# Norms of the RWKV keys by block-of-ones matmuls, in a hybrid RWKV-7 and MoBA layer on one core

## The chip, the cores and the metric

The kernel runs on one core of one Trainium2 chip. The metric is the device time of one execution in microseconds, as the median of the runs. Engines are named as the profile names them: PE is TensorE's matmuls and PEld its weight loads, DVE is VectorE, ACT is ScalarE, POOL is GpSimd, SP is SyncE.

## The reference, cut to what matters

One decoder layer on 256 tokens of width 2048: a shared RMS norm, one input projection of 12416 columns, two token mixers side by side, two gated projections back to 2048, an output projection and a residual. The change lies in the RWKV-7 mixer, which has 16 heads of 64 channels. Its keys are scaled and normalised per head:

```python
    kk = (k * k_k).reshape(B, S, H, N).astype(f32)
    kk = kk / jnp.maximum(jnp.sqrt(jnp.sum(kk * kk, axis=-1, keepdims=True)), 1e-12)
    k = k * (1.0 + (a - 1.0) * k_a)
    ...
    bh = kk * ah
    ...
    def step(state, inp):
        r_t, w_t, k_t, v_t, kk_t, b_t = inp
        sa = jnp.einsum('bhvk,bhk->bhv', state, -kk_t)
        state = (state * w_t[:, :, None, :]
                 + sa[..., None] * b_t[:, :, None, :]
                 + v_t[..., None] * k_t[:, :, None, :])
        y_t = jnp.einsum('bhvk,bhk->bhv', state, r_t)
        return state, y_t
```

## The kernel before

**Main work.** Every projection is a product of an fp32 weight with activations that are held as two fp32r parts, xh and xl. A weight half of 128 x 1024 is split on the fly: ScalarE copies it to fp32r (hi, L216), VectorE subtracts that from the original (lo, L222), and TensorE does three passes, hi with xh, hi with xl, lo with xh. Channel-major chunks (mm_fm, L314) take 24 matmuls of 256 columns for a weight half, token-major chunks (mm_tm, L334; the queries, keys and values of MoBA) 12 of 512 columns. A job is one weight half. The loop run_jobs (L253) prepares the halves two jobs ahead; hi and lo have three buffers each, and the raw weights two buffers of two halves.

**Side work.** After each job, pump (L199) advances generators that hold everything else: the RWKV elementwise work (rwkv_elem, L405), the score matmuls (rwkv_r, L511), the inversion of triangular 32 x 32 blocks on VectorE (inverse, L557), the state recursion (rwkv_v), attention (moba). The 16 heads are worked in two groups g of 8; tiles have channels on the partitions, two heads to a tile of 128, four tiles fi for a group, and 256 tokens in the columns. The first jobs are ordered by hand (L294); for all the rest a scheduler of the tile framework decides the order of each engine's instructions when the program is built. At run time every engine works strictly in that order.

**The key norms (L453 to L509).** kk is k times k_k (L459), and sq its square (L461), in the first half of a tile named bk (sn in the code). Eight matmuls take 128 columns of sq as weights and a two-column selector sel2 as the moving side (L467), which gives sums with tokens on the partitions, 128 x 16. Square root (L469), maximum (L470) and reciprocal (L471) run on these 16 columns. A copy spreads each norm over 64 columns (L473) in the second half of the tile, eight transposes turn that back to channels on the partitions (L481), and kk is multiplied by it from PSUM (L485). Then ar is kk times a decay (L490), t1 and k follow (L494, L497), a becomes -kk a (L499), and a new tile of the same slot, bk, is filled: one half by VectorE from a (L507), the other by GpSimd from k (L508). The score matmuls (L534) take bk and ar. head_sums (L396) is a helper that sums over heads with a block-diagonal matrix of ones, bones, and leaves each sum on all 64 channels; before, only rwkv_tr used it (L633, matmuls at L401).

Of the kernel before, what the change touches and what calls it, by code (L numbers as in the profile page):

```python
# [10 lines left out]
F32R = mybir.dt.float32r  # L11
BF16 = mybir.dt.bfloat16
U8 = mybir.dt.uint8
AF = mybir.ActivationFunctionType
ALU = mybir.AluOpType
AX = mybir.AxisListType

P = 128
D = 2048
S = 256  # L20
# [16 lines left out]
def tile_hybrid_block(ctx: ExitStack, tc: tile.TileContext, x, pv, wdu, wau,  # L37
                      w_in, w_pr, w_pm, w_out, out):
    nc = tc.nc
    act, dve, pool, pe, sp = nc.scalar, nc.vector, nc.gpsimd, nc.tensor, nc.sync  # L40
# [10 lines left out]
    def nm(s):  # L51
        cnt[0] += 1
        return f"{s}_{cnt[0]}"

    def T(tag, shape, dt=F32, bufs=1):
        return sb.tile(shape, dt, tag=tag, name=nm(tag), bufs=bufs)
# [4 lines left out]
    def PSS():  # L61
        return psd.tile([P, 512], F32, tag="ps", name=nm("ps"))

    def C(name, shape, dt=F32):
        return cp.tile(shape, dt, tag=name, name=name)

    def f32(ap):
        return ap.bitcast(F32)
# [12 lines left out]
    ident = C("ident", [P, P])  # L81
# [23 lines left out]
    pool.memset(mone[0:64, 0:64], 1.0)  # L105
    pool.memset(mone[64:128, 64:128], 1.0)
    dve.tensor_copy(bones, mone)
    sel2 = C("sel2", [P, 2])
    pool.memset(sel2, 0.0)
    pool.memset(sel2[0:64, 0:1], 1.0)  # L110
    pool.memset(sel2[64:128, 1:2], 1.0)
    rst = C("rst", [P, 16, 65], BF16)
    pool.memset(rst, 1.0)
    pool.memset(rst[:, :, 0:1], 0.0)
# [281 lines left out]
    def head_sums(ps, parts, half):  # L396

        for i in range(2):
            fs = slice((2 * half + i) * S, (2 * half + i + 1) * S)
            for u in range(2):  # L400
                pe.matmul(ps[:, i * S:(i + 1) * S], bones, parts[u][:, fs], start=(u == 0),  # L401
                          stop=(u == 1))


    def rwkv_elem(g):  # L405
        r = R[g]
        lr = T("ep", [P, 2, 512])
        for i, src in enumerate((wdu, wau)):
            for sl in (slice(0, 64), slice(64, 128)):
                act.dma_start(lr[sl, i, :], src[:, g * 512:(g + 1) * 512])  # L410
        yield
        yield
        th = T("bk", [P, 2, 512], F32R)
        lw = T("lora", [P, 2, 512], F32R)
        act.activation(th[64:128], lr[64:128], AF.Copy)
        act.activation(lw[0:64], lr[0:64], AF.Copy)
        dve.tensor_tensor(lw[64:128], lr[64:128], f32(th[64:128]), ALU.subtract)
        yield
        sg = T("sg", [P, 4, 4, 65])
        a = T("a", [P, 4, S])  # L420
        pool.memset(sg[:, :, :, 0:1], 0.0)
        for half in range(2):
            pw, pa = PSS(), PSS()
            for i in range(2):
                fi = 2 * half + i
                col = 4 * g + fi
                fs = slice(fi * P, (fi + 1) * P)
                for j, ps in enumerate((pw, pa)):
                    o = ps[:, i * S:(i + 1) * S]
                    pe.matmul(o, lw[:, j, fs], xx[:, 2 * j, :], start=True, stop=False)  # L430
                    pe.matmul(o, lw[:, j, fs], xx[:, 2 * j + 1, :], start=False, stop=True)
                act.activation(sg[:, fi, :, 1:65],
                               pw[:, i * S:(i + 1) * S].rearrange("p (c t) -> p c t", c=4),
                               AF.Sigmoid, bias=PV[:, PV_W0 + col:PV_W0 + col + 1])
                act.activation(a[:, fi, :], pa[:, i * S:(i + 1) * S], AF.Sigmoid,
                               bias=PV[:, PV_A0 + col:PV_A0 + col + 1])
            yield
        cs = T("cs", [P, 16, 65])
        dve.tensor_tensor_scan(cs.rearrange("p a b -> p (a b)"), rst.rearrange("p a b -> p (a b)"),
                               sg.rearrange("p f c t -> p (f c t)"), 0.0, ALU.mult, ALU.add)  # L440
        yield
        cc = T("sg", [P, 16, 65])
        dve.tensor_tensor(cc, cs, cs[:, :, 32:33].to_broadcast([P, 16, 65]), ALU.subtract)
        yield
        ep = T("ep", [P, 4, 4, 65])
        em = T("cs", [P, 4, 4, 65])
        act.activation(ep.rearrange("p f c t -> p (f c) t"), cc, AF.Exp, scale=-LAM)
        act.activation(em.rearrange("p f c t -> p (f c) t"), cc, AF.Exp, scale=LAM)
        fac = T("fac", [P, 4, 3])
        dve.tensor_tensor(fac, ep[:, :, 0:3, 64], em[:, :, 1:4, 0], ALU.mult)  # L450
        r["fac"] = fac
        yield
        k = r["k"]  # L453
        kk = T("kk", [P, 4, S])
        sn = T("bk", [P, 2, 1024])
        sq = sn[:, 0, :].rearrange("p (f t) -> p f t", f=4)
        for fi in range(4):
            col = 4 * g + fi
            dve.tensor_scalar(kk[:, fi, :], k[:, fi, :], PV[:, PV_KK + col:PV_KK + col + 1], None,  # L459
                              ALU.mult)  # L460
        act.activation(sq, kk, AF.Square)  # L461
        yield
        pn = PSS()
        pn4 = pn[:, 0:16].rearrange("p (c f e) -> p c f e", c=2, f=4)
        for c in range(2):
            for fi in range(4):
                pe.matmul(pn4[:, c, fi, :], sq[:, fi, c * P:(c + 1) * P], sel2, start=True, stop=True)  # L467
        n = T("n", [P, 16])
        act.activation(n, pn[:, 0:16], AF.Sqrt)  # L469
        dve.tensor_scalar(n, n, 1e-12, None, ALU.max)  # L470
        dve.reciprocal(n, n)  # L471
        nx = sn[:, 1, :].rearrange("p (a b) -> p a b", b=64)
        dve.tensor_copy(nx, n.rearrange("p (a o) -> p a o", o=1).to_broadcast([P, 16, 64]))  # L473
        yield
        yield
        for half in range(2):
            pb = PSS()
            for i in range(2):
                fi = 2 * half + i
                for c in range(2):  # L480
                    pe.transpose(pb[:, i * S + c * P:i * S + (c + 1) * P],  # L481
                                 nx[:, c * 8 + 2 * fi:c * 8 + 2 * fi + 2, :].rearrange(
                                     "p a b -> p (a b)"), ident)
            v = kk[:, 2 * half:2 * half + 2, :].rearrange("p f t -> p (f t)")
            dve.tensor_tensor(v, v, pb, ALU.mult)  # L485
        yield
        ar = T("ar", [P, 4, 4, 2, 64])
        r["ar"], r["ep"] = ar, ep
        kk4 = kk.rearrange("p f (c t) -> p f c t", c=4)
        dve.tensor_tensor(ar[:, :, :, 0, :], kk4, ep[:, :, :, 0:64], ALU.mult)  # L490
        t1 = sq
        for fi in range(4):
            col = 4 * g + fi
            dve.tensor_scalar(t1[:, fi, :], a[:, fi, :], -1.0, PV[:, PV_KA + col:PV_KA + col + 1],  # L494
                              ALU.add, ALU.mult)
        yield
        dve.scalar_tensor_tensor(k, t1, 1.0, k, ALU.add, ALU.mult)  # L497
        yield
        dve.scalar_tensor_tensor(a, kk, -1.0, a, ALU.mult, ALU.mult)  # L499
        yield  # L500
        bk = T("bk", [P, 4, 4, 2, 64])
        r["bk"] = bk
        a4 = a.rearrange("p f (c t) -> p f c t", c=4)
        k4 = k.rearrange("p f (c t) -> p f c t", c=4)
        for p in range(2):
            sl = slice(64 * p, 64 * p + 64)
            dve.tensor_tensor(bk[sl, :, :, p, :], a4[sl], em[sl, :, :, 1:65], ALU.mult)  # L507
            pool.tensor_tensor(bk[sl, :, :, 1 - p, :], k4[sl], em[sl, :, :, 1:65], ALU.mult)  # L508
            yield  # L509
# [513 lines left out]
    for g in range(2):  # L1023
        c = 512 * g
        chunk(w_in, C_K + c, 512, KT, fm_x, shift_post("k", "k", g, PV_MUK, 8))
        post = shift_post("r", "r", g, PV_MUR, 0)
        if g == 0:
            chunk(w_in, C_WD, 128, KT, fm_x, then(wa_post, (rwkv_elem(0), "e0")))
        else:
            post = then(post, (rwkv_elem(1), "e1"))  # L1030
        chunk(w_in, C_R + c, 512, KT, fm_x, then(post, (rwkv_r(g), f"r{g}")))
        vp = then(shift_post("v", "v", g, PV_MUV, 16), (rwkv_mid(g), f"i{g}"), (rwkv_v(g), f"v{g}"))
        chunk(w_in, C_V + c, 512, KT, fm_x, with_need("v0", vp) if g else vp)
        qp = qk_post("q", g)
        chunk(w_in, C_Q + c, 512, KT, tm_x, with_need("m0", qp) if g else qp)
        chunk(w_in, C_KQ + c, 512, KT, tm_x, qk_post("k", g))
        chunk(w_in, C_VQ + c, 512, KT, tm_x, then(vq_post(g), (moba(g), f"m{g}")))
# [63 lines left out]
```

## Time and profile before

| | |
|---|---|
| median of 3 runs | 836.4 us (835.27 to 838.43) |
| profiled execution | 836.63 us |
| its span, first to last instruction | 834.9 us |
| granted TensorE clock, mean | 0.998 |
| PE, PEld | 98%, 91% of the span |
| DVE, ACT, POOL | 66%, 51%, 3% of the span |

A row of the profile names a source line, an engine, an operation, and out<-in with tile names; times are in microseconds, the mean of one instruction in ns. Matmuls are pipelined, so that a single one shows a longer time than the distance to the next. In brackets stands how long the engine sat idle before and what released it.

### The profile page before, as it was taken

The numbers are of one execution on the slowest core, as the hardware profiler recorded it, in microseconds if no ns is written. First come the engines' busy times: TensorE is split into PE (matmuls) and PEld (weight loads), VectorE is DVE, ScalarE is ACT, GpSimd is POOL, SyncE is SP. The second block draws the span as 40 slices with busy tenths as digits, with TensorE's granted clock in tenths as the row PEclk, the third lists the DMA queues.
The fourth block names the chain that finished last, engine by engine and source line by source line (L and its number), as shares of the span: only waits on it lengthen the run. The fifth ranks groups of instructions, "written<-read, shape, count | busy, mean of one in ns | idle before, by whom it ended". The sixth has DMA issues, their size and how long they took to land.

```text
span 834.9 us, 15904 instructions
## 1 busy us (share of the span) xinstructions
PE 821.7 (98%) x6770; PEld 763.3 (91%) x6770; DVE 550.3 (66%) x776; ACT 423.4 (51%) x568; POOL 28.9 (3%) x42
## 2 busy tenths in 40 slices
PE   8999999999999999999989999999999999999998
PEld 8999878899998788899989998899999999998887
DVE  5769958956569649769955578644554566665553
ACT  6785435544437576445434467654444444443332
POOL 5001200000000002000000000000000000000000
PEclk9999999999999999999999999999999999999999
DMA  8564555664434444455673324566555555556772
GB/s 305 179 199 153 178 163 165 201 177 153 150 108 142 158 152 152 156 173 187 200 220 105 106 98 151 177 202 198 186 184 193 201 186 169 201 176 203 249 231 99
DMA packets 83207, 145.78 MB, mean 175 GB/s; under 512 B 11568, under 2 KB 13872, under 8 KB 83136
## 3 DMA queue, kind: packets, MB, share of 16 engines
q1 hardware_dynamic: 71584, 138.55, 51.2%
q10 hardware_dynamic: 11520, 6.16, 2.7%
q8 instruction: 53, 0.87, 0.4%
q14 instruction: 18, 0.15, 0.1%
q0 software_dynamic: 32, 0.05, 0.0%
HBM read 141.61 MB, written 3.15 MB: 173 GB/s over the span
## 4 chain that ended last, share of the span: by engine, by line
PE 92%; ACT 3%; DVE 2%; DMA 2%; issue 1%; SPq 0%; ACTq 0%; DVEq 0%
PE pm L329 56%; PE pm L348 9%; PE pm L347 9%; PE pm L349 9%; PE ps L534 1%; PE ps L672 1%; PE ps L679 1%; ACT bk L849 1%; PE ps L878 1%; DMA td<-kk 1%; DMA cs<-td 1%; PE ps L831 1%; PE ps L696 1%; DVE lo L222 1%; ACT hi L216 1%
## 5 line engine op out<-in xcount | busy, mean ns | idle before, releaser
L222 DVE TENSOR_TENSOR lo<-raw,hi 128x1024 fp32r<-128x1024 f32 (+1 forms) x259 | 316.3, 1225 | 212.9 <-ACT hi L216 212.0
L216 ACT ACTIVATE hi<-raw 128x1024 fp32r<-128x1024 f32 (+1 forms) x259 | 272.6, 1055 | 339.1 <-PE pm L329 193.1
L329 PE MATMUL pm<-xh,hi 128*128 128x256 f32 x1168 | 326.8, 282 | 0.4 <-ACT xh L144 0.4
L329 PE MATMUL pm<-xl,hi 128*128 128x256 f32 x1168 | 324.9, 280 | 0.0
L329 PE MATMUL pm<-xh,lo 128*128 128x256 f32 x1168 | 323.9, 280 | 1.0 <-DVE lo L222 1.0
L329 PEld LDWEIGHTS pm<-xh,hi 128*128 128x128 f32 x1168 | 220.4, 190 | 3.2 <-issue 0.8
L329 PEld LDWEIGHTS pm<-xh,lo 128*128 128x128 f32 x1168 | 220.0, 190 | 2.6 <-DVE lo L222 1.4
L329 PEld LDWEIGHTS pm<-xl,hi 128*128 128x128 f32 x1168 | 220.8, 190 | 1.0 <-issue 0.3
L348 PE MATMUL pm<-lo,xh 128*128 128x512 f32 x192 | 76.3, 397 | 0.0
L349 PE MATMUL pm<-hi,xl 128*128 128x512 f32 x192 | 75.5, 393 | 0.0
L347 PE MATMUL pm<-hi,xh 128*128 128x512 f32 x192 | 74.1, 401 | 0.0
L348 PE MATMUL pm<-lo,mgh 128*128 128x512 f32 (+1 forms) x128 | 48.4, 378 | 0.0
L349 PE MATMUL pm<-hi,mgl 128*128 128x512 f32 (+1 forms) x128 | 48.0, 376 | 0.0
L347 PE MATMUL pm<-hi,mgh 128*128 128x512 f32 (+1 forms) x128 | 44.4, 377 | 0.0
L349 PEld LDWEIGHTS pm<-hi,xl 128*128 128x128 f32 x192 | 36.1, 188 | 7.8 <-issue 0.2
L348 PEld LDWEIGHTS pm<-lo,xh 128*128 128x128 f32 x192 | 36.1, 188 | 7.7 <-DVE lo L222 0.6
L347 PEld LDWEIGHTS pm<-hi,xh 128*128 128x128 f32 x192 | 35.9, 188 | 7.8 <-issue 0.5
L347 PEld LDWEIGHTS pm<-hi,mgh 128*128 128x128 f32 x128 | 24.0, 188 | 4.7
L349 PEld LDWEIGHTS pm<-hi,mgl 128*128 128x128 f32 x128 | 24.0, 188 | 4.7
L348 PEld LDWEIGHTS pm<-lo,mgh 128*128 128x128 f32 x128 | 24.0, 188 | 4.4
L566 DVE TENSOR_TENSOR tmp<-sg,kk 64x31 f32<-64x31 f32 (+15 forms) x62 | 20.6, 331 | 4.6 <-DMA sg<-gd 3.5
L329 PE MATMUL pm<-bk,hi 128*128 128x256 f32 x128 | 22.8, 281 | 0.0
(275 smaller groups left out, 990.6 us busy)
## 6 DMA issues: line engine op xcount, KB each, us to landing
raw<-in_w_in_dram SPq DMA_DIRECT2D x94, 1024.0 KB, 5.0
raw<-in_w_out_dram SPq DMA_DIRECT2D x16, 1024.0 KB, 5.6
raw<-in_w_proj_moba_dram SPq DMA_DIRECT2D x8, 1024.0 KB, 5.1
raw<-in_w_proj_rwkv_dram SPq DMA_DIRECT2D x8, 1024.0 KB, 5.2
raw<-in_w_in_dram SPq DMA_DIRECT2D x5, 512.0 KB, 6.4
k<-in_x_dram ACTq DMA_DIRECT2D x4, 256.0 KB, 5.3
r<-in_x_dram ACTq DMA_DIRECT2D x4, 256.0 KB, 4.6
k<-in_x_dram SPq DMA_DIRECT2D x2, 256.0 KB, 4.8
```

The lines of the kernel that those rows point to most:

```text
L216: act.activation(job["hi"][:, c], job["src"][:, c], AF.Copy)
L222: dve.tensor_tensor(job["lo"][:, c], job["src"][:, c], f32(job["hi"][:, c]), ALU.subtract)
L329: pe.matmul(o, (hi, hi, lo)[ps][:, i, cs], (mh, ml, mh)[ps](k), start=(k == 0 and fi % 2 == 0 and ps == 0), stop=(k == jb["last"] and ps = ...
L347: pe.matmul(o, sh[:, k, ts], hi[:, i, cs], start=(k == 0), stop=False)
L348: pe.matmul(o, sh[:, k, ts], lo[:, i, cs], start=False, stop=False)
L349: pe.matmul(o, sl[:, k, ts], hi[:, i, cs], start=False, stop=end)
L534: pe.matmul(pss[p][:, c * P:(c + 1) * P], bk[sl, fi, c].rearrange("p a t -> p (a t)"), ar[sl, fi, c].rearrange("p a t -> p (a t)"), start= ...
L566: dve.tensor_tensor(tv, gcol.to_broadcast([64, nt, j + 1]), trow.to_broadcast([64, nt, j + 1]), ALU.mult)
L672: pe.matmul(ps[64 * p:64 * p + 64, c0 + 64 * fi:c0 + 64 * fi + 64], LL[p][:, fi, c, which, :], UV[:, c, p, fi, :], start=(fi == 0), stop=( ...
L679: pe.matmul(ps[sl, c0 + 64 * fi:c0 + 64 * fi + 64], ar[sl, fi, c, which, :], St[sl, fi, :], start=False, stop=True, skip_group_check=True)
L696: pe.matmul(ps[sl, cols], X64[sl, fi * 4 + c, :], Zs[sl, cols], start=True, stop=True)
L831: pe.matmul(pss[p][:, i * nk:(i + 1) * nk], q[rows, fi, 0:P] if u == 0 else q[rows, fi, P:S], k[rows, fi, 0:nk], start=True, stop=True)
```

## The change

The squares are split in two fp32r parts: a ScalarE copy (sqh) and a VectorE subtraction (sql). head_sums multiplies both parts by the block of ones, so that each channel row receives the sum of its own head. Square root, maximum, reciprocal and the multiplication then run on all 128 x 512 of a half, in channel-major layout. The selector, the two-column sums, the spreading copy and the transposes go.

```diff
-    sel2 = C("sel2", [P, 2])
-    pool.memset(sel2, 0.0)
-    pool.memset(sel2[0:64, 0:1], 1.0)
-    pool.memset(sel2[64:128, 1:2], 1.0)
...
-        pn = PSS()
-        pn4 = pn[:, 0:16].rearrange("p (c f e) -> p c f e", c=2, f=4)
-        for c in range(2):
-            for fi in range(4):
-                pe.matmul(pn4[:, c, fi, :], sq[:, fi, c * P:(c + 1) * P], sel2, start=True, stop=True)
-        n = T("n", [P, 16])
-        act.activation(n, pn[:, 0:16], AF.Sqrt)
-        dve.tensor_scalar(n, n, 1e-12, None, ALU.max)
-        dve.reciprocal(n, n)
-        nx = sn[:, 1, :].rearrange("p (a b) -> p a b", b=64)
-        dve.tensor_copy(nx, n.rearrange("p (a o) -> p a o", o=1).to_broadcast([P, 16, 64]))
-        yield
+        sqv = sq.rearrange("p f t -> p (f t)")
+        sqh, sql = (T(t, [P, 1024], F32R) for t in ("sg", "ar"))
+        act.activation(sqh, sqv, AF.Copy)
+        dve.tensor_tensor(sql, sqv, f32(sqh), ALU.subtract)
         yield
         for half in range(2):
-            pb = PSS()
-            for i in range(2):
-                fi = 2 * half + i
-                for c in range(2):
-                    pe.transpose(pb[:, i * S + c * P:i * S + (c + 1) * P],
-                                 nx[:, c * 8 + 2 * fi:c * 8 + 2 * fi + 2, :].rearrange(
-                                     "p a b -> p (a b)"), ident)
+            pn = PSS()
+            head_sums(pn, (sqh, sql), half)
+            n = sn[:, 1, 512 * half:512 * half + 512]
+            act.activation(n, pn, AF.Sqrt)
+            dve.tensor_scalar(n, n, 1e-12, None, ALU.max)
             v = kk[:, 2 * half:2 * half + 2, :].rearrange("p f t -> p (f t)")
-            dve.tensor_tensor(v, v, pb, ALU.mult)
+            dve.reciprocal(n, n)
+            dve.tensor_tensor(v, v, n, ALU.mult)
```

The scheduler makes a new order for the whole program from this. Lines of the changed kernel are 4 lower than before up to L458 and 12 lower from the line after the edit (L478 is L490 of before, L218 is L222, L487 is L499, L495 is L507, L502 is L514, L507 is L519, L522 is L534). Three places matter.

VectorE in group 0, from the norms to the second operand of the scores (lo, raw and hi are the weight halves; bk the tile of the norms). Before:

```order
L473 COPY bk_873<-n_920 128x1024
L519 SCALAR_TENSOR_TENSOR r_859<-r_859,pv,k_489 128x256
L222 TENSOR_TENSOR lo_997<-raw_879,hi_995 128x1024
L222 TENSOR_TENSOR lo_1033<-raw_953,hi_1031 128x1024
L485 TENSOR_TENSOR kk_872<-kk_872,ps_983 128x512
L485 TENSOR_TENSOR kk_872<-kk_872,ps_989 128x512
L490 TENSOR_TENSOR ar_1023<-kk_872,ep_825 128x16x64
L499 SCALAR_TENSOR_TENSOR a_675<-kk_872,a_675 128x1024
L222 TENSOR_TENSOR lo_1062<-raw_953,hi_1060 128x1024
L507 TENSOR_TENSOR bk_1119<-a_675,cs_826 64x16x64 x2
```

And with the change:

```order
L472 RECIPROCAL bk_869<-bk_869 128x512
L218 TENSOR_TENSOR lo_995<-raw_875,hi_993 128x1024
L472 RECIPROCAL bk_869<-bk_869 128x512
L502 TENSOR_TENSOR ar_987<-r_855,ep_821 128x16x64
L218 TENSOR_TENSOR lo_1026<-raw_957,hi_1024 128x1024
L473 TENSOR_TENSOR kk_868<-kk_868,bk_869 128x512
L218 TENSOR_TENSOR lo_1055<-raw_957,hi_1053 128x1024
L473 TENSOR_TENSOR kk_868<-kk_868,bk_869 128x512
L507 SCALAR_TENSOR_TENSOR r_855<-r_855,pv,k_485 128x256 x4
L218 TENSOR_TENSOR lo_1088<-raw_1022,hi_1086 128x1024
L478 TENSOR_TENSOR ar_987<-kk_868,ep_821 128x16x64
L487 SCALAR_TENSOR_TENSOR a_671<-kk_868,a_671 128x1024
```

Each reciprocal now stands directly ahead of lo halves; from the start of the lo half whose first use is at the main matmul 458 (460 now) to L507, the list has nine lo halves where it had seven. Behind the first reciprocal stands the half that is first used at the main matmul 556, behind the second those first used at 582, 606, 626 and 638.

VectorE in group 1, the same piece. Before:

```order
L222 TENSOR_TENSOR lo_3563<-raw_3477,hi_3561 128x1024
L795 TENSOR_TENSOR qkn_3448<-pm_3251,ssk_3449 128x512
L795 TENSOR_TENSOR qkn_3448<-pm_3252,ssk_3449 128x512
L485 TENSOR_TENSOR kk_3425<-kk_3425,ps_3513 128x512
L485 TENSOR_TENSOR kk_3425<-kk_3425,ps_3519 128x512
L222 TENSOR_TENSOR lo_3582<-raw_3525,hi_3580 128x1024
L490 TENSOR_TENSOR ar_3555<-kk_3425,ep_3401 128x16x64
L499 SCALAR_TENSOR_TENSOR a_3287<-kk_3425,a_3287 128x1024
L222 TENSOR_TENSOR lo_3599<-raw_3525,hi_3597 128x1024
L222 TENSOR_TENSOR lo_3620<-raw_3578,hi_3618 128x1024
L507 TENSOR_TENSOR bk_3613<-a_3287,cs_3402 64x16x64 x2
```

And with the change:

```order
L218 TENSOR_TENSOR lo_3571<-raw_3519,hi_3569 128x1024
L783 TENSOR_TENSOR qkn_3440<-pm_3243,ssk_3441 128x512
L783 TENSOR_TENSOR qkn_3440<-pm_3244,ssk_3441 128x512
L472 RECIPROCAL bk_3418<-bk_3418 128x512 x2
L218 TENSOR_TENSOR lo_3590<-raw_3519,hi_3588 128x1024
L218 TENSOR_TENSOR lo_3610<-raw_3567,hi_3608 128x1024
L218 TENSOR_TENSOR lo_3627<-raw_3567,hi_3625 128x1024
L473 TENSOR_TENSOR kk_3417<-kk_3417,bk_3418 128x512 x2
L478 TENSOR_TENSOR ar_3513<-kk_3417,ep_3393 128x16x64
L487 SCALAR_TENSOR_TENSOR a_3279<-kk_3417,a_3279 128x1024
L495 TENSOR_TENSOR bk_3585<-a_3279,cs_3394 64x16x64 x2
```

Both reciprocals stand in one run, ahead of three lo halves and of everything that leads to L507. The last half ahead of them, lo_3571, has its first use at the main matmul 1754, the next three at 1770, 1780 and 1802.

TensorE in group 1, where the score matmuls (ps<-ar,bk) begin. Before:

```order
L329 MATMUL pm_3663<-xh,hi_3636 128x256
L329 MATMUL pm_3663<-xl,hi_3636 128x256
L534 MATMUL ps_3754<-ar_3555,bk_3613 128x128
L329 MATMUL pm_3662<-xh,lo_3638 128x256
L329 MATMUL pm_3662<-xh,hi_3636 128x256
```

And with the change:

```order
L325 MATMUL pm_3655<-xh,lo_3627 128x256
L522 MATMUL ps_3712<-ar_3513,bk_3585 128x128 x4
L325 MATMUL pm_3654<-xh,hi_3650 128x256
L325 MATMUL pm_3654<-xl,hi_3650 128x256
L522 MATMUL ps_3713<-ar_3513,bk_3585 128x128 x4
```

Counted in main matmuls, the scores of group 1 begin behind 1824 with the change (one single one stood behind 1804 before, the next behind 1828) and end behind 1896 (1920 before). In group 0 they begin behind 650 (626 before, with a second lot behind 650) and end behind 696 (708 before). The sums stand behind 460 and 480, and 1706 and 1718, where the two-column sums stood behind 456 and 1680.

## Rows read from the trace of the kernel before

**Rows 1.** Busy time of each engine, its share of the span, and instructions, from the page.

```profile
PE 821.7 (98%) x6770; PEld 763.3 (91%) x6770; DVE 550.3 (66%) x776; ACT 423.4 (51%) x568; POOL 28.9 (3%) x42
```

**Rows 2.** Stretches: us, then PE, PEld, DVE, ACT, POOL busy (instructions), clock, DMA share, GB/s.

```profile
81.00:91.00 10.00, 9.04 (x75) 8.61 (x74) 9.93 (x7) 4.24 (x4) 6.38 (x4) 1.00 0.49 149
...
316.00:327.00 11.00, 11.00 (x49) 8.83 (x49) 10.38 (x21) 9.91 (x11) 0.00 (x0) 1.00 0.29 88
```

**Rows 3.** Timeline of PE around the first late lo half: start, us, line, instructions, idle before.

```profile
88.96 0.39 PE L329 MATMUL pm<-xh,lo 128*128 128x256 f32 x1 [0.96 <-DVE lo L222]
...
91.45 1.16 PE L534 MATMUL ps<-ar,bk 64*128 64x128 f32 x14
```

**Rows 4.** The chain that ended last, in order of time: start us, us, what.

```profile
67.44 1.68 PE ps L467 x16
...
98.37 0.65 PE ps L534 x8
...
327.60 0.87 PE ps L481 x8
...
340.80 2.83 PE pm L329 x24
...
346.98 0.64 PE ps L534 x6
...
374.84 0.48 PE ps L401 x4
```

**Rows 5.** Groups by shape on ACT: out<-in xcount | busy us, mean ns | idle before.

```profile
L216 ACT ACTIVATE hi<-raw 128x1024 fp32r<-128x1024 f32 x257 | 271.4, 1059 | 335.3 <-PE pm L329 193.1 <-PE pm L349 41.5 <-DMA raw<-in_w_in_dram 30.8
...
L865 ACT ACTIVATE ar<-ps 128x512 f32<-128x512 f32 x12 | 6.9, 586 | 0.8 <-PE ps L863 0.6
```

**Rows 6.** Groups by shape on DVE, columns as in rows 5.

```profile
L222 DVE TENSOR_TENSOR lo<-raw,hi 128x1024 fp32r<-128x1024 f32 x257 | 314.9, 1229 | 212.5 <-ACT hi L216 211.6
...
L494 DVE TENSOR_SCALAR bk<-a,pv 128x256 f32<-128x256 f32 x8 | 2.5, 351 | 0.0
...
L473 DVE COPY bk<-n 128x1024 f32<-128x1024 f32 x2 | 1.4, 693 | 0.0
...
L856 DVE RECIPROCAL smx<-smx 128x2 f32<-128x2 f32 x8 | 1.3, 163 | 2.4 <-ACT bk L849 2.3
...
L394 DVE RECIPROCAL st<-st 128x8 f32<-128x8 f32 x4 | 0.8, 200 | 3.2 <-ACT st L393 3.2
...
L471 DVE RECIPROCAL n<-n 128x16 f32<-128x16 f32 x2 | 0.5, 249 | 0.0
...
L470 DVE TENSOR_SCALAR n<-n 128x16 f32<-128x16 f32 x2 | 0.3, 172 | 0.0
```

**Rows 7.** Timelines of POOL in group 0 and in group 1.

```profile
81.32 5.36 POOL L508 TENSOR_TENSOR bk<-k,cs 64x1024 f32<-64x1024 f32 x2 [67.41 <-PE pm L329]
...
328.61 5.06 POOL L508 TENSOR_TENSOR bk<-k,cs 64x1024 f32<-64x1024 f32 x2 [68.60 <-PE ps L481]
```

**Rows 8.** Timeline of DVE in group 0, columns as in rows 3.

```profile
80.78 1.29 DVE L485 TENSOR_TENSOR kk<-kk,ps 128x512 f32<-128x512 f32 x2 [0.83 <-PE ps L481]
82.10 2.51 DVE L490 TENSOR_TENSOR ar<-kk,ep 128x1024 f32<-128x1024 f32 x1
84.53 3.23 DVE L499 SCALAR_TENSOR_TENSOR a<-kk,a 128x1024 f32<-128x1024 f32 x1
...
88.82 2.46 DVE L507 TENSOR_TENSOR bk<-a,cs 64x1024 f32<-64x1024 f32 x2
```

**Rows 9.** Timeline of DVE in group 1.

```profile
331.60 3.15 DVE L222 TENSOR_TENSOR lo<-raw,hi 128x1024 fp32r<-128x1024 f32 x1
334.68 1.21 DVE L490 TENSOR_TENSOR ar<-kk,ep 128x1024 f32<-128x1024 f32 x1
335.81 1.21 DVE L499 SCALAR_TENSOR_TENSOR a<-kk,a 128x1024 f32<-128x1024 f32 x1
...
339.22 2.46 DVE L507 TENSOR_TENSOR bk<-a,cs 64x1024 f32<-64x1024 f32 x2
```

**Rows 10.** Who waited for whom on PE: total us, times, longest.

```profile
PE ps L595 <- DMA cs<-td: 2.2, 1, 2.2
```

## Prediction

> **What bounds the kernel now.** I read the busy shares first, then TensorE's waits, then the stretches around the two places that the change edits, then VectorE's and GpSimd's timelines there. TensorE is busy 98% of the span, VectorE 66% [rows 1]. So a microsecond that TensorE loses is lost for good, and one that VectorE gains is worth nothing by itself, unless TensorE waits for it there. The average hides that VectorE is full exactly where the keys are normalised: 9.93 us of 10 in 81 to 91 us (group 0), 10.38 of 11 in 316 to 327 us (group 1) [rows 2]. In that first stretch TensorE already waits 0.96 us for one lo half that VectorE delivers late [rows 3]. The reader should see that the change takes work from the full TensorE and gives more to the engine that is full there.
>
> **TensorE's part.** Per group it loses eight two-column sums, which show as 16 passes over 1.68 us, and eight transposes, 0.87 us; it gains eight block-of-ones matmuls of 256 columns, of the kind whose four take 0.48 us, so 0.96 us [rows 4]. That is 1.59 us saved per group, 3.2 us in all, and the most that the change can win from the array directly.
>
> **ScalarE's part.** Added per group: two 512-wide Sqrt from PSUM at about 0.59 us, the price of the 512-wide PSUM copy [rows 5], and one 1024-wide Copy, at most twice that, in place of one small Sqrt. ScalarE is half idle [rows 1]; I cost this at nothing. What covers it: the two square roots come behind two hi splits and are needed only when VectorE reaches the maxima, and VectorE gets there later than they do. If that cover fails, it is about 2 us per group.
>
> **VectorE's part**, per group. Removed: the 16-column maximum (0.17 us) and reciprocal (0.25), and the spreading copy (0.69) [rows 6]. Added: one 1024-wide subtraction, as a lo split, 1.23 us [rows 6]; two 512-wide maxima: 172 ns at 16 columns and 351 at 256 [rows 6] give 0.75 ns a column, so 0.54 us each; and two 512-wide **reciprocals**. The trace shows no wide one. Narrow ones take 163, 200 and 249 ns at 2, 8 and 16 columns [rows 6]: 6.1 ns a column on a straight line, eight times the maximum's price. At 512 that is 249 ns + 496 x 6.1 ns = 3.28 us. Bounds: below, the price per column of a maximum, 0.54 us; above, 249/16 = 15.6 ns for every column with no fixed part, 8.0 us. I take 3.28, because three points lie on the line. The Trainium skill (VectorE: DVE Perf Modes, "First, the fixed hardware budget") speaks against this change: it says that a reciprocal is an iterated divide with a repeat count of 8. Eight cycles at that page's 0.96 GHz would be an estimate of 4.3 us, and the sum below would be 4 us higher; the rows here give 6.1 ns, nearer six cycles, so the rows' figure stands.
>
> The final multiply reads the norms from SBUF in place of PSUM, which changes its own time little. But the norms now lie in the tile whose slot the bk tile takes, so GpSimd's two bk products, which started as soon as the transposes were done and took 5.36 and 5.06 us [rows 7], now wait for the last key multiply, and run beside operations with both operands in SBUF. Beside them the ar and a products took 2.51 and 3.23 us in group 0 [rows 8] where they took 1.21 each alone in group 1 [rows 9], 3.3 us lost; in group 1 one lo split took 3.15 us [rows 9], 1.9 lost. I take 3.3 us in both groups now.
>
> **The sum, group 0.** The score matmuls (L534) need the bk products (L507), which end at 88.82 + 2.46 = 91.28 us [rows 8]. Ahead of them the new VectorE order has: two more lo splits (2.46), the subtraction (1.23), one more 512-wide normalising multiply (half a split, 0.6), the maxima (1.08 - 0.17), the reciprocals (6.56 - 0.25), less the copy (0.69): 10.8 us. Neighbours overlap by 0.08 us (the ar product ends at 84.61, the next starts at 84.53 [rows 8]); nine more instructions take off 0.7. The wait of 0.83 us for the transposes [rows 8] goes. So L507 ends 9.3 us later, at 100.6 us. In the new order TensorE starts the score matmuls one weight half later, where it was at 98.37 us before [rows 4], after 1.16 us of score matmuls that it now has still to do [rows 3]: 97.2 us. The shift is **+3.4 us**. Without wait it would have come there at 97.2 - 0.96 - 1.59 = 94.7, so its wait grows from 0.96 to about 6 us, most of it for lo halves that stand behind a reciprocal. TensorE's saving is swallowed by that wait.
>
> **The sum, group 1.** L507 ended at 339.22 + 2.46 = 341.68 us [rows 9]. Ahead of it come one more lo split (1.23), the subtraction (1.23), maxima and reciprocals as above (0.91 + 6.31), less the copy (0.69): 9.0, less 0.4 for overlaps; GpSimd's hindrance 3.3 in place of 1.9; and about 0.5 us more idle, since the order puts the sums behind the exponentials: 10.5 us, end at 352.2. Here both reciprocals stand in one run ahead of three lo halves. TensorE reached the score matmuls at 346.98 us, four matmuls and one score matmul later than they start in the new order; at 2.83 us for 24 [rows 4] that point was at 346.4. The shift is **+5.8 us**; the wait is about 7.4 us where there was none.
>
> Later stages I leave as they are. The new order is one weight half ahead with the last score matmuls in both groups, which gives back 2.7 us of the delay to the chain of the triangular inverses, while TensorE itself comes 3.4 and 9.2 us later; the 2.2 us that TensorE waits for the inverse [rows 10] should stay near that.
>
> Sum: +9.2 us on the profiled execution's 836.6 us, 845.8; the median of the runs, 836.4, is 0.2 us below it, so **845.6 us**. The likeliest case's own range is 840 to 849.5: low with no hindrance by GpSimd and no added idle (-3.3 in group 0, -1.9 in group 1), high with 2 us of ScalarE's part uncovered in each group.
>
> **Rivals.**
> *Not slower: the reciprocals fit in.* Each must take at most 3.28 - 9.2/4 = 1.0 us for the shift to vanish; at 0.54 us L507 ends 5.5 us earlier in each group, group 0 then gains about 2 us and group 1 is at zero, or gains its 1.59 where VectorE has caught up: 832.8 to 834.5 us. For it: every other 512-wide operation here takes 0.7 us or less. Against it: the straight line of the narrow rows. Chance 0.14.
> *The wide reciprocal is dearer.* Each further microsecond of one is 4 us of time, since four of them stand on the path: a third dearer, at 4.4 us, 850; at the upper bound, 8.0 us, 864.5. For it: narrow rows measure a price per column over only 14 columns; against it, again the line. The Trainium skill's repeat count (same page and section) would be this case. Chance 0.12.
> *The inverse chain is late as well.* The new order puts the inverse's first matmuls (L595) 20 main matmuls (2.4 us) earlier on TensorE in group 1. If the chain keeps the whole 10.5 us while TensorE comes only 5.8 later, the wait of 2.2 us [rows 10] grows by 4.7 + 2.4 = 7.1 us: 853. Against it: the last score matmuls are one weight half earlier. Chance 0.12.
> That the change does not do what it says is no rival: the order shows its instructions in their places.
>
> **Chances.** Forecast 0.52, the three rivals 0.14, 0.12, 0.12, and 0.10 for mixtures in which half of the delay is absorbed by waits that are there already (836 to 841). About 0.5%, 4.2 us, is what a measurement of this kernel can tell from no change. Slower by more than that: 0.52 + 0.12 + 0.12 = 0.76. Of the not-slower rival most lies within 0.5%, as do the mixtures: 0.16 within, 0.08 faster. The range is 838 to 855: it leaves out the not-slower rival and the far end of the dear reciprocal; the lowest price of a reciprocal lies outside it, since only that rival has it.
>
> **What the new profile would show.** Four RECIPROCAL rows of 512 columns near 3.3 us; TensorE's waits for lo halves and for the bk products of about 6 us before 105 us and 7 us before 355 us; VectorE without a gap from 65 to 100 us; the block-of-ones matmuls at 0.12 us each and no two-column sums; GpSimd's products starting behind the last key multiply. I am wrong if the reciprocals take under 1.0 us, or if they take 3.3 us and TensorE shows no new wait: then the lo halves had slack that I did not see. If the waits are there but TensorE waits longer at the inverse, the third rival holds.

## The result, and the profile after

| | before | after |
|---|---|---|
| median of 4 runs | 836.5 us (835.3 to 838.4) | 849.0 us (847.2 to 849.9) |
| profiled execution | 836.6 us | 848.1 us |
| its span | 834.9 us | 846.4 us |
| granted TensorE clock, mean | 0.998 | 0.991 |

The changed kernel takes 1.0144 times as long, 95% interval 1.0117 to 1.0171: 12 us slower (11.5 us between the two spans), where +9.2 us was forecast.

The busy shares from the page, to set against [rows 1]:

```profile
PE 823.2 (97%) x6738; PEld 764.1 (90%) x6738; DVE 567.6 (67%) x780; ACT 421.7 (50%) x569; POOL 29.5 (3%) x39
```

VectorE has gained 17 us of work in all. Most of it is the wide reciprocals (groups by shape on VectorE, columns as in rows 5):

```profile
L472 DVE RECIPROCAL bk<-bk 128x512 f32<-128x512 f32 x4 | 13.2, 3326 | 0.0
```

The waits of TensorE, in us in total, times, and longest. The row of the inverse (L583) looks like that of [rows 10], but it stands in the other group, as shown below:

```profile
PE pm L344 <- DVE lo L218: 4.6, 3, 3.8
PE pm L343 <- ACT hi L212: 3.5, 1, 3.5
...
PE pm L325 <- DVE lo L218: 2.8, 3, 1.1
PE ps L583 <- DMA cs<-td: 2.7, 1, 2.7
PE ps L522 <- POOL kk L542: 1.9, 1, 1.9
```

These sum to 15.5 us. Before, the waits of that size behind the start were the 0.96 and 2.2 us of [rows 3, 10] and, at the attention, one more:

```profile
PE ps L863 <- ACT hi L216: 1.6, 1, 1.6
```

That is 4.8 us, so TensorE waits 10.7 us more.

**Group 0.** VectorE's timeline (columns as in rows 3), to set against [rows 8]:

```profile
75.38 3.35 DVE L472 RECIPROCAL bk<-bk 128x512 f32<-128x512 f32 x1
78.64 1.16 DVE L218 TENSOR_TENSOR lo<-raw,hi 128x1024 fp32r<-128x1024 f32 x1
79.72 3.34 DVE L472 RECIPROCAL bk<-bk 128x512 f32<-128x512 f32 x1
...
87.52 5.55 DVE L507 SCALAR_TENSOR_TENSOR r<-r,pv,k 128x256 f32<-128x256 f32 x4
...
98.13 2.46 DVE L495 TENSOR_TENSOR bk<-a,cs 64x1024 f32<-64x1024 f32 x2
```

The bk product ends at 98.13 + 2.46 = 100.59 us (forecast 100.6). TensorE's timeline there has four gaps, 5.1 us in all:

```profile
79.85 0.39 PE L325 MATMUL pm<-xh,lo 128*128 128x256 f32 x1 [0.75 <-DVE lo L218]
...
86.50 0.74 PE L343 MATMUL pm<-hi,xh 128*128 128x512 f32 x2 [3.55 <-ACT hi L212]
...
94.25 0.50 PE L344 MATMUL pm<-lo,xh 128*128 128x512 f32 x1 [0.41 <-DVE lo L218]
...
97.66 0.50 PE L344 MATMUL pm<-lo,xh 128*128 128x512 f32 x1 [0.38 <-DVE lo L218]
```

The long one waits for a hi half, and ScalarE's timeline says why that was late:

```profile
85.39 1.06 ACT L212 ACTIVATE hi<-raw 128x1024 fp32r<-128x1024 f32 x1 [5.75 <-DMA raw<-in_w_in_dram]
```

Its raw weights had not landed. By the buffers' order they take the slot of the raw tile whose last reader is the lo half at 78.64 us, directly behind the first reciprocal. The DMA queue of SyncE bears that out: it issues this transfer when that lo half ends, at 79.80 us.

```profile
79.83 0.37 SPq L231 DMA_DIRECT2D raw<-in_w_in_dram  x1
```

So VectorE's delay came round to TensorE through a raw buffer, a DMA and ScalarE.

**Group 1.** VectorE and GpSimd, to set against [rows 7, 9], and then TensorE:

```profile
339.78 6.55 DVE L472 RECIPROCAL bk<-bk 128x512 f32<-128x512 f32 x2
346.25 3.42 DVE L218 TENSOR_TENSOR lo<-raw,hi 128x1024 fp32r<-128x1024 f32 x3
...
352.05 3.24 DVE L487 SCALAR_TENSOR_TENSOR a<-kk,a 128x1024 f32<-128x1024 f32 x1
355.33 4.35 DVE L495 TENSOR_TENSOR bk<-a,cs 64x1024 f32<-64x1024 f32 x2
```

```profile
351.05 6.29 POOL L496 TENSOR_TENSOR bk<-k,cs 64x1024 f32<-64x1024 f32 x2 [86.13 <-DVE kk L473]
357.40 0.94 POOL L541 MEMSET kk<- 64x1024 f32 x1
358.40 0.15 POOL L542 MEMSET kk<- 64x32 f32 x1
```

```profile
347.46 0.80 PE L344 MATMUL pm<-lo,xh 128*128 128x512 f32 x1 [3.77 <-DVE lo L218]
...
358.57 1.13 PE L522 MATMUL ps<-ar,bk 64*128 64x128 f32 x8 [1.91 <-POOL kk L542]
```

Three lo halves stand behind both reciprocals, and TensorE waits 3.77 us for the first. The profile puts the second wait down to GpSimd's last memset, whose tile the scores don't read; it ended at about that moment. The two instructions of L495 by themselves (duration in ns least/median/most, first and last start) and the loads of the scores show what was really late:

```profile
L495 DVE TENSOR_TENSOR bk<-a,cs x2: 1221/2160/3099, 355.3 to 358.5; 64x1024 f32<-64x1024 f32 x2
```

```profile
L522 PEld LDWEIGHTS ps<-ar,bk x41: 182/188/289, 358.5 to 370.0; 64*128 64x128 f32 x41
```

Each of the two fills half of the partitions of bk, and the first four score matmuls (eight records) read the half that comes first. Beside GpSimd the first took 3.10 us, not 1.22, and ended at 355.33 + 3.10 = 358.43 us, just ahead of the first load. So this wait is one for VectorE's bk product, as forecast. It is no longer than what GpSimd added to L487 and L495 (2.0 and 1.9 us), and e5_bk_vector, without GpSimd's products, doesn't have it.

**The clock.** The same three waits are followed by a second loss. Windows of the changed kernel around them (us, then PE, PEld, DVE, ACT, POOL busy, granted clock, DMA share, GB/s):

```profile
86.50:88.00 1.50, 1.50 (x10) 1.40 (x11) 1.50 (x4) 0.00 (x0) 0.25 (x1) 0.93 0.00 0
88.00:90.00 2.00, 2.00 (x11) 2.00 (x11) 2.00 (x1) 0.00 (x0) 2.00 (x1) 0.50 0.93 242
90.00:92.00 2.00, 2.00 (x15) 2.00 (x14) 2.00 (x2) 1.06 (x1) 1.93 (x2) 0.70 0.73 283
...
349.00:351.00 2.00, 2.00 (x7) 1.57 (x6) 1.97 (x4) 0.17 (x1) 0.00 (x0) 0.59 0.89 324
...
360.00:365.00 5.00, 5.00 (x30) 4.72 (x29) 5.00 (x6) 1.72 (x2) 0.00 (x0) 0.66 0.36 92
```

TensorE stood for 3.55 us, worked on for about 1.3 us at the full level (2.4 GHz), and was then granted the lower one (1.2 GHz), although it was busy the whole time; full speed came back at about 91.2 us. Two rows of its timeline, the first in that stretch and the second behind it, with the start of the next matmul 0.21 us after the one and 0.12 us after the other:

```profile
88.36 0.42 PE L325 MATMUL pm<-xl,hi 128*128 128x256 f32 x1
...
91.41 0.28 PE L325 MATMUL pm<-xh,lo 128*128 128x256 f32 x1
```

Some 15 matmuls at 0.1 us more each are 1.5 us. In group 1 the same happens behind the wait of 3.77 us, seven matmuls of 512 columns at 0.43 in place of 0.23 us (1.4 us), and behind the wait for the bk product, (1 - 0.66) x 5 us = 1.7 us. Together 4.6 us.

**The inverse.** TensorE's wait for the inverse is followed by such a stretch in both kernels, but it isn't in the same place. In the kernel before it is in group 1, and group 0 has none; in the changed kernel it is in group 0, and group 1 has none. Before, then after:

```profile
437.11 1.19 PE L595 MATMUL ps<-cs,LL 32*32 32x32 f32 x32 [2.21 <-DMA cs<-td]
```

```profile
188.63 1.17 PE L583 MATMUL ps<-cs,LL 32*32 32x32 f32 x32 [2.68 <-DMA cs<-td]
```

And the windows behind them, two before and one after:

```profile
435.00:440.00 5.00, 2.89 (x41) 2.85 (x42) 2.91 (x3) 1.73 (x3) 0.00 (x0) 0.85 0.48 107
440.00:445.00 5.00, 5.00 (x77) 4.87 (x77) 4.56 (x7) 1.47 (x2) 0.00 (x0) 0.81 0.66 213
```

```profile
190.00:195.00 5.00, 5.00 (x33) 4.87 (x33) 3.68 (x6) 1.49 (x2) 0.00 (x0) 0.66 0.44 142
```

The lower clock takes 1.7 us in each, so in the total these two cancel.

**The budget.** Saved on the array as forecast, -3.2; waits, +10.7; clock, +4.6: +12.1, against +11.5 between the spans. Where it arose, by the same terms:

- Group 0, up to its scores: waits 5.1 - 1.0, clock 1.5, saved 1.6: +4.0 us.
- The inverse of group 0: wait 2.7, clock 1.7: +4.4.
- Group 1, up to its scores: waits 3.8 + 1.9, clock 1.4 + 1.7, saved 1.6: +7.2.
- Behind that: two late lo halves in 375 to 420 us, +2.0; the inverse of group 1 without its wait and its clock, -2.2 - 1.7; the attention without its wait, -1.6: -3.5.

A count of main matmuls in the two traces bears this out for group 0. The 450th, ahead of its sums, starts 0.7 us earlier than before; the 1680th, ahead of the sums of group 1, at 321.32 us where it was 313.85, 7.5 us later.

### The profile page after: what moved, and what is told of

Read it like the earlier page. It is cut to its first block, busy times and chain, and to the rows that moved or that the text cites. A ratio compares the mean times of both kernels' runs of the same rounds, so it can differ in the third digit from the quotient of the medians.

```text
span 846.4 us, 15839 instructions
## 1 busy us (share of the span) xinstructions
PE 823.2 (97%) x6738; PEld 764.1 (90%) x6738; DVE 567.6 (67%) x780; ACT 421.7 (50%) x569; POOL 29.5 (3%) x39
## 4 chain that ended last, share of the span: by engine, by line
PE 84%; DVE 7%; DMA 4%; issue 2%; ACT 1%; POOL 1%; SPq 0%; ACTq 0%; POOLq 0%; DVEq 0%
PE pm L325 52%; PE pm L343 7%; PE pm L345 7%; PE pm L344 7%; DVE lo L218 2%; DMA raw<-in_w_in_dram 1%; PE ps L522 1%; PE ps L660 1%; PE ps L819 1%; PE ps L866 1%; DVE bk L472 1%; ACT hi L212 1%; PE ps L667 1%; POOL bk L496 1%; DMA sg<-gd 1%
## 5 line engine op out<-in xcount | busy, mean ns | idle before, releaser
L218 DVE TENSOR_TENSOR lo<-raw,hi 128x1024 fp32r<-128x1024 f32 (+1 forms) x259 | 314.4, 1217 | 214.5 <-ACT hi L212 209.2
L343 PEld LDWEIGHTS pm<-hi,xh 128*128 128x128 f32 x192 | 36.2, 190 | 11.5 <-ACT hi L212 3.7
```

The lines of the kernel that those rows point to most:

```text
L218: dve.tensor_tensor(job["lo"][:, c], job["src"][:, c], f32(job["hi"][:, c]), ALU.subtract)
L343: pe.matmul(o, sh[:, k, ts], hi[:, i, cs], start=(k == 0), stop=False)
```

## The experiments

Ratios are to the kernel before, run beside it on the same chip; its median was 837.3 us for the first four, 836.3 for the next four and 834.7 for the last two, so the ratios are what compares. They are not quite the quotients of these medians.

| | ratio (95% interval) | median |
|---|---|---|
| changed kernel | 1.0144 (1.0117 to 1.0171) | 849.0 |
| e1_no_recip | 0.9986 (0.9964 to 1.0008) | 835.0 |
| e2_wide_before | 1.0137 (1.007 to 1.0205) | 848.7 |
| e3_norm_other_slot | 1.012 (1.0055 to 1.0184) | 844.3 |
| e4_ln_exp | 1.0107 (1.005 to 1.0164) | 846.9 |
| e5_bk_vector | 1.009 (1.0063 to 1.0118) | 844.9 |
| e6_ln_exp_bk_vector | 1.0045 (1.0027 to 1.0063) | 840.0 |
| e7_before_bk_vector | 1.0008 (0.9996 to 1.0021) | 837.2 |
| e8_quarter_reciprocals | 1.0122 (1.0098 to 1.0146) | 846.9 |
| e9_ln_bias_bk_vector | 1.0052 (1.0035 to 1.007) | 839.3 |
| e10_ln_bias | 1.0078 (1.005 to 1.0107) | 841.4 |

**e1_no_recip.** The change, with a plain multiply in the place of the inversion.

```diff
-            dve.reciprocal(n, n)
+            dve.tensor_scalar(n, n, 1e-6, None, ALU.mult)
```

> The changed kernel with the four wide reciprocals left out: a multiplication by a constant of the same 128 x 512 shape stands in their place, so the keys are multiplied by the norm and not divided by it. The order on TensorE and VectorE differs from the changed kernel's in some 30 rows only. Theory (the reciprocals stand on the path, 4 us of time for 1 us of each, and TensorE's waits and its clock follow from them): a multiplication takes 0.4 to 0.6 us in place of 3.35 us, VectorE ends the bk products about 5.6 us earlier in each group, TensorE's waits for lo halves, for the hi half and for GpSimd nearly vanish, the granted clock is 1.00 in all stretches; 833 to 836 us. Rival (the time comes from the other work on VectorE, from GpSimd's late start, or from the new order as such): it keeps most of the 12 us, 843 us or more.

Measured 0.9986: no difference from before, at a mean clock of 0.996. The waits did not all vanish: 4.3 us for lo halves are left, which the saving on the array pays for, and the 2.7 us for the inverse of group 0, with none in group 1. So that wait belongs to the new order and not to the reciprocals. The reciprocals, or what they push past its slack, are the whole of the loss.

**e2_wide_before.** The other way round: the kernel before, with its narrow reciprocal moved behind the spreading copy.

```diff
-        dve.reciprocal(n, n)
...
         dve.tensor_copy(nx, n.rearrange("p (a o) -> p a o", o=1).to_broadcast([P, 16, 64]))
+        for half in range(2):
+            dve.reciprocal(sn[:, 1, 512 * half:512 * half + 512], sn[:, 1, 512 * half:512 * half + 512])
```

> The kernel before, with the 16-column reciprocal taken out and two 512-wide reciprocals put behind the spreading copy: two-column sums, transposes and all else as before, the result the same. Theory: each reciprocal takes 3.3 us here too; VectorE's path to the bk products is 6.3 us longer in each group, of which group 0 passes on nearly all and group 1 three to six, 845 to 849 us, with TensorE waiting for lo halves in both groups. Rival (the block-of-ones sums, the split of the squares and the order make the loss): 836 to 840 us.

Measured 1.0137, as much as the change by the median, though the interval is wide (6 to 17 us). The transposes, which need the spread norms, now wait for the reciprocal itself (TensorE's timeline):

```profile
83.23 1.54 PE L482 MATMUL ps<-ident,bk 128*128 128x128 f32 x6 [2.71 <-DVE bk L474]
```

So wide reciprocals cost this kernel some 11 us without any block of ones, squares in two parts or new layout. They do so by other waits than I expected: 5.7 us at the transposes, 2.6 for lo halves, and 4.6 at the inverse of group 1 in place of 2.2.

**e3_norm_other_slot.** The change, with the norms in a tile of their own slot, so that GpSimd's products no longer wait for the key multiply.

```diff
+        pns = [PSS(), PSS()]
         for half in range(2):
-            pn = PSS()
-            head_sums(pn, (sqh, sql), half)
-            n = sn[:, 1, 512 * half:512 * half + 512]
-            act.activation(n, pn, AF.Sqrt)
+            head_sums(pns[half], (sqh, sql), half)
+        nn = T("sg", [P, 2, 512])
+        for half in range(2):
+            n = nn[:, half, :]
+            act.activation(n, pns[half], AF.Sqrt)
```

> The changed kernel with the norms in the slot of the split squares (sg) instead of the slot that bk takes, so GpSimd need not wait for the last key multiply. TensorE's order is that of the changed kernel row for row, VectorE's too but for names. Theory: VectorE is full all through this stretch, so GpSimd hinders it by about the same 4 us per group wherever it runs, unless it runs beside a reciprocal; 845 to 849 us. Rival (GpSimd's late start is itself on the path, since TensorE waits for GpSimd in group 1): 3 to 5 us less, 843 to 846 us, and no wait of TensorE for GpSimd.

The ratio, 1.012, does not separate it from the change. The profile does say where the collision went: GpSimd starts at 72.31 us, and VectorE's two maxima beside it take 4.54 us where they took 0.92 in the changed kernel.

```profile
72.31 5.40 POOL L498 TENSOR_TENSOR bk<-k,cs 64x1024 f32<-64x1024 f32 x2 [58.28 <-DVE k L487]
```

```profile
73.45 4.54 DVE L472 TENSOR_SCALAR sg<-sg 128x512 f32<-128x512 f32 x2 [0.17 <-ACT sg L471]
```

The wait at the scores is gone, and TensorE waits 4.36 us for a lo half in its stead. Moving the collision earlier did not remove it.

**e4_ln_exp.** The change, with the inverse root as exp(-0.5 ln x) on ScalarE.

```diff
-            act.activation(n, pn, AF.Sqrt)
-            dve.tensor_scalar(n, n, 1e-12, None, ALU.max)
+            dve.tensor_scalar(n, pn, 1e-24, None, ALU.max)
+            act.activation(n, n, AF.Ln)
+            act.activation(n, n, AF.Exp, scale=-0.5)
...
-            dve.reciprocal(n, n)
```

> The changed kernel with the inverse root computed on ScalarE, as exp of minus half the logarithm of the sum; VectorE keeps only the maximum, now from PSUM, and the multiplication. Theory: VectorE sheds 6.7 us per group and adds 0.4, ScalarE gains two Ln and two Exp of about 0.6 us and one or two table loads of 1.28 us, with room for them; TensorE has 1.6 us less work per group than before the change: 832 to 837 us. Rival (order or the other work): 843 us or more.

A miss: 1.0107, though 13.2 us of VectorE's work are gone. TensorE still waits 6.4 us for lo halves, 5.4 of them in one gap. VectorE's timeline ahead of it:

```profile
80.87 5.55 DVE L507 SCALAR_TENSOR_TENSOR r<-r,pv,k 128x256 f32<-128x256 f32 x4
```

The four r products collide with GpSimd here as in the change, and stand in front of the lo halves. But e1_no_recip had the same collision in the same place:

```profile
79.71 5.56 DVE L507 SCALAR_TENSOR_TENSOR r<-r,pv,k 128x256 f32<-128x256 f32 x4
```

There TensorE waited 2.53 us behind it, for a lo half that comes directly after the r products. In e4_ln_exp the ar and a products (L478, L487, 1.21 us each) stand between the two, and VectorE had first stood idle for the exponential:

```profile
77.39 0.69 DVE L473 TENSOR_TENSOR kk<-kk,bk 128x512 f32<-128x512 f32 x1 [2.00 <-ACT bk L471]
```

That makes the theory wider: the reciprocals are not the only thing that delays a lo half. The collision, the order behind it and the longer way through ScalarE can delay one too, and this run can't tell them apart. Three further runs on the collision follow.

**e5_bk_vector.** The change, with GpSimd's products on VectorE.

```diff
-            pool.tensor_tensor(bk[sl, :, :, 1 - p, :], k4[sl], em[sl, :, :, 1:65], ALU.mult)
+            dve.tensor_tensor(bk[sl, :, :, 1 - p, :], k4[sl], em[sl, :, :, 1:65], ALU.mult)
```

> The changed kernel with GpSimd's two products of k into bk (L496) done by VectorE; nothing else differs. Theory (beside the wide reciprocals, GpSimd's products slow VectorE's operations on SBUF, 3.9 us per group, and in group 1 TensorE's score products wait 1.9 us for them): the four r products (L507) fall from 5.55 us to about 1.7, the bk product (L495) from 4.35 to 2.5, VectorE gains two products of 1.2 us per group, and the time falls by 3 to 6 us to 843-846. Rival (the reciprocals are all of it, and VectorE is what is short): the two more products add their 2.4 us per group, 848-853.

Measured 1.009: about 4.5 us come back (the intervals of the two ratios just touch) by giving the scarcer engine more to do. VectorE's timeline:

```profile
88.13 1.67 DVE L507 SCALAR_TENSOR_TENSOR r<-r,pv,k 128x256 f32<-128x256 f32 x4
...
93.12 2.44 DVE L496 TENSOR_TENSOR bk<-k,cs 64x1024 f32<-64x1024 f32 x2
```

The r products fell from 5.55 to 1.67 us, the added products cost 2.44, and the wait at the scores of group 1 is gone (it was put down to GpSimd's memset, as said above, when this was expected). The Trainium skill (SBUF — State Buffer, "Who interferes with whom") has VectorE share one pair of SBUF ports with GpSimd under an exclusive lock; the 5.55 and 1.67 us agree.

**e6_ln_exp_bk_vector.** Both together.

> The logarithm and exponential of e4_ln_exp in place of square root and reciprocal, and GpSimd's products on VectorE too. Theory (what kept e4_ln_exp at 847 was GpSimd's products in front of the lo halves): no reciprocal and no collision are left, so 835-841, with TensorE waiting less than 2.5 us for lo halves in the two groups together. Rival (it was the new table loads and ScalarE, or the longer way round through ScalarE): 845-849, with TensorE still waiting for hi or lo halves.

Measured 1.0045, so the theory holds for the time: the two causes together make about 8 of the 12 us. Its waits were more than expected: 3.1 us for lo halves in group 0 and 1.0 in group 1, and 5.1 at the two inverses.

**e7_before_bk_vector.** The same move of the products in the kernel before.

> The kernel before with GpSimd's products of k into bk on VectorE. Theory: in the kernel before the collision is paid too, but its VectorE has room ahead of the end of a group, so the time moves little, 833-838. Rival (VectorE has no room in the kernel before either): the 2.4 us per group come on top, 839-842.

Measured 1.0008: no difference. There the ar and a products take 1.23 and 1.22 us in place of the 2.51 and 3.23 of [rows 8], but in the kernel before no lo half was late by more than 0.96 us, so there was little to win.

**e8_quarter_reciprocals.** The change, with each reciprocal in four.

```diff
-            dve.reciprocal(n, n)
+            for u in range(4):
+                w = slice(128 * u, 128 * u + 128)
+                dve.reciprocal(n[:, w], n[:, w])
```

> The changed kernel with each 128x512 reciprocal cut into four of 128x128: the same columns, in instructions of about 0.85 us. Theory (it is the total that VectorE has to do ahead of the lo halves): the same time as the change, 847-851. Rival (it is the length of the one instruction that a lo half waits behind): 842-846.

```profile
L474 DVE RECIPROCAL bk<-bk 128x128 f32<-128x128 f32 x16 | 13.4, 904 | 0.0
```

The pieces add up to 13.4 us where it was 13.2, and the scheduler left the four of a half in one run, so the length of a block was not really tried. The time, 1.0122, overlaps with that of the change, and the long waits are the same: 3.3 us for a hi half in group 0, 3.8 for a lo half in group 1. This run settles little.

**e9_ln_bias_bk_vector** and **e10_ln_bias.** As e6_ln_exp_bk_vector, with the bound of the norms as a bias of the logarithm, which saves VectorE the maxima; in the second, GpSimd keeps its products.

```diff
+    epsk = C("epsk", [P, 1])
+    pool.memset(epsk, 1e-24)
...
-            dve.tensor_scalar(n, pn, 1e-24, None, ALU.max)
-            act.activation(n, n, AF.Ln)
+            act.activation(n, pn, AF.Ln, bias=epsk)
             act.activation(n, n, AF.Exp, scale=-0.5)
```

> As e6_ln_exp_bk_vector, and the lower bound of the norms put into the logarithm as a bias of 1e-24, so that VectorE's two maxima (0.68 us each) go as well. Theory (what is left of the change's cost is VectorE's own work ahead of the lo halves): VectorE now has about as much to do there as in the kernel before, TensorE's waits for lo halves in the two groups fall under 1.5 us, and the time to 834-838. Rival (the longer way through ScalarE with its table loads, or the new order, costs what is left): 839-842, with waits for lo halves as in e6_ln_exp_bk_vector or for hi halves in their place.

> As e9_ln_bias_bk_vector, with the two products of k left on GpSimd. Theory: only the collision with GpSimd is left, 2 to 4 us over e9_ln_bias_bk_vector: 837-842. Rival (the collision costs as much as from e6_ln_exp_bk_vector to e4_ln_exp, 7 us): 842-846.

Measured 1.0052 and 1.0078. For the first the rival came out: no better than e6_ln_exp_bk_vector. VectorE now stands idle, with lo halves queued behind the instruction that waits:

```profile
75.88 0.69 DVE L474 TENSOR_TENSOR kk<-kk,bk 128x512 f32<-128x512 f32 x1 [2.55 <-ACT bk L472]
```

```profile
71.34 1.28 ACT L471 ACT_TABLE_LOAD   x1
72.64 1.27 ACT L471 ACTIVATE bk<-ps,epsk 128x512 f32<-128x512 f32 x2
73.92 1.28 ACT L472 ACT_TABLE_LOAD   x1
```

Two table loads of 1.28 us and the two activations put the norms later than VectorE gets to them, and TensorE waits 3.2 us for a hi half in group 0 and 2.7 for a lo half in group 1. The collision is worth 2.1 us here by the medians, but the two intervals overlap. None of the versions that compute the norms beats the kernel before: the 3.2 us saved on the array never came to more than what the inversion in channel-major layout cost elsewhere.

## Why the prediction was right, point by point

The direction, the mechanism and the two places were as forecast; the time, 849.0 us, lies in the range and 3.4 us above the forecast. By the terms of the budget group 0 cost 4.0 us up to its scores where 3.4 were forecast, and group 1 7.2 where it was 5.8. The later stages, which it left as they were, nearly cancel.

- **The wide reciprocal.** Forecast 3.28 us from a straight line through three narrow rows, measured 3.33 (x4). Over 32 times the longest narrow row the line held. The Trainium skill's repeat count of 8 (VectorE: DVE Perf Modes, "First, the fixed hardware budget"), an estimate of 8.3 ns a column at its 0.96 GHz, disagrees: (3326 - 249) / 496 = 6.2 ns here.
- **The shift of the bk product in group 0.** Forecast end 100.6, measured 100.59 us. That is partly luck: GpSimd's hindrance came as 3.9 us (5.55 - 1.67, the time in e5_bk_vector), not 3.3, and on the r products, where I had named ar and a.
- **The array's saving.** The block-of-ones matmuls come at 0.12 us each, as forecast.
- **The sizes of the waits.** Forecast 6 and 7.4 us, measured 5.1 and 3.77 + 1.91 = 5.7. I had said that most of group 0's wait would be for lo halves behind a reciprocal. It was for a hi half, behind a raw buffer that such a lo half held. My sum followed VectorE's queue to the scores only, and not the two-deep raw buffers back to ScalarE.
- **The term that was missing: the clock.** The sum priced a wait at its length. Each of the three long waits was also followed by a stretch at the lower clock, 4.6 us in all. This is the step that failed. The waits of the two groups came out 2.6 us below the forecast, so without the clock the two groups would have cost 6.6 us and not 9.2; the two errors partly cancel.
- **"Later stages I leave as they are."** Their sum stayed near nothing, +4.4 - 3.5 = 0.9 us, but that is luck. The 2.2 us for the inverse did not stay: group 1 lost its wait and group 0 got one of 2.7 us. The forecast saw that the inverse of group 1 comes 20 main matmuls earlier on TensorE; that of group 0 does too, behind 1036 where it stood behind 1056, and there the wait came. Besides, two lo halves in 375 to 420 us were late by 2.0 us in all, and the 1.6 us wait of the attention went.
- **GpSimd's hindrance.** Forecast 3.3 us in both groups. In group 1 L487 took 3.24 and L495 4.35 us, 3.9 more than alone (1.21 and 2.46 in [rows 9]).
- **The rivals.** "The reciprocals fit in" and "the wide reciprocal is dearer" fell with 3.33 us. "The inverse chain is late" fell in group 1, where no wait for it is left; what it describes, an inverse that comes too early for its data, happened in group 0, at 4.4 us with the clock. e1_no_recip shows how near the first was: at a reciprocal of no more than a multiply the change is at zero.

What stays open: the split of the 12 us between reciprocals and collision. They do not add up: taking away the one gives 13 us, the other 4.5, replacing the one by ScalarE's work 3. Nor is either of them free by itself: the reciprocals without the collision cost 7.5 us (e5_bk_vector), and the collision without the reciprocals cost nothing in e1_no_recip and in the kernel before, but 5 us between e4_ln_exp and e6_ln_exp_bk_vector. Open, too, is why the new order moved the inverse's wait from group 1 to group 0.

## What to carry to other kernels

When an operation changes its layout, count columns per partition: the norms went from 16 columns to 1024 per group, and an operation that costs 6 ns a column turned from nothing into 6.6 us. On an engine that feeds the bound one through an in-order queue, price what stands behind the added work, back through the buffers that it holds as well as forward; and add to a long wait of TensorE what the clock can take afterwards. Compare waits place by place: a total that hardly moved, 2.2 and 2.7 us for the inverse, hid one wait that went and one that came. Before moving more onto a full VectorE, look at what GpSimd runs beside it: moving GpSimd's work over can be the cheaper way.

## What the runs showed that I had not expected

- In the changed kernel four waits of 1.9 to 3.8 us each were followed by 3 to 4 us at the lower clock level, which began between just before TensorE resumed (group 1, 347.2 us) and 2.3 us after (at the scores). In the kernel before, the 2.2 us for the inverse were, the 0.96 us for a lo half were not. The length of a wait does not settle it: in e1_no_recip one of 2.53 us was followed by none, one of 2.7 us by more than 5 us (a clock of 0.50 in all of 185 to 190 us).
- Beside GpSimd's products a VectorE operation can stretch by more than three times: the four r products of 1.67 us took 5.55, two maxima of 0.92 us took 4.54. An operation that only reads one operand from SBUF, the maximum, was hit as hard as those with two.
- GpSimd's own products stretch too, from 4.63 us in group 0 to 6.29 in group 1 of the same run.
